# A hybrid decoder layer on one core: the lo parts of all weight tiles, on VectorE or on GpSimd

## The chip, the cores and the metric

The kernel runs on one core of a Trainium2 chip. The engines that matter are TensorE (in the profile PE for its matmuls and PEld for its weight loads), VectorE (DVE), ScalarE (ACT), GpSimd (POOL) and SyncE (SP), which here issues most DMAs; names that end in q are an engine's queue. The metric is the device time of one execution in microseconds. Before the change three runs took 1840.11, 1841.65 and 1845.51 us; the median is 1841.65.

## What is computed

One layer with three token mixers side by side, on 2048 tokens of width 1024, in fp32. Cut to what matters:

```python
hn = rms_norm(x, pre_norm_w)
u = hn @ w_in                                   # 1024 -> 5392 columns, split
y_ssd  = ssd_mixer(z, xbc, dt, ...)             # conv of 4 taps, chunked state space, gated norm
y_conf = conformer_conv(conf_in, ...) * silu(conf_gate)   # conv of 31 taps, layer norm
y_attn = sliding_window_attention(q, k, v, ...) * silu(attn_gate)
y = concatenate([y_ssd, y_conf, y_attn])        # 2048 columns
h = x + rms_norm(y @ w_out, post_norm_w)
out = h + (p @ ple_proj) * sigmoid(h @ ple_gate)
```

## The kernel before

Everything is kept transposed: 128 channels on the partitions, 512 tokens (one of four chunks) in a row. The four large products (w_in, w_out, ple_gate, ple_proj) are made in a reduced-precision fp32 format of TensorE, called fp32r in the profile. To keep fp32 accuracy both factors are split in two: hi is the value rounded to fp32r, lo is what the rounding left. A product is then three matmuls, hi by lo, lo by hi and hi by hi, added up in one PSUM tile (lines 443 to 445, 1048 to 1050, and 207 to 209).

Weights come in tiles of 128 rows by 1024 numbers (512 KB; for ple_proj 128 by 256). `load_w` fetches one into a staging buffer `wst`, of which there are two (line 196, a DMA on SyncE's queue), has ScalarE write `whi` (line 190, a CAST) and VectorE subtract to get `wlo` (line 191, inside the helper `split`). There are five buffers each for `whi` and `wlo`. A `wst` buffer is free again when the subtraction has read it; only then can SyncE issue the load of the tile after next. `split` serves the activations too, which is why line 191 also stands for `al` and `bl` in the profile. The one tile named dt has its own code (`dt_tile`, lines 459 to 461) with its own small subtraction on VectorE.

The program has three stages, which follow each other on TensorE:

- Stage 1, to about 1240 us: two halves of two chunks each. In each half the 17 units of work in a list (A attention, C conformer, S state space, G a new group) load their two or three weight tiles, project both chunks with them (`proj`), and leave the rest of their work to generators that are advanced between the projections. The conformer's convolution needs 30 VectorE instructions for each tile of two chunks (line 691, one per tap), dealt out between the others.
- Stage 2, to about 1619 us: for each of four chunks 16 weight tiles of w_out, 24 matmuls per tile; beside them the norms of the next chunk (`stats`, `prep`) and, after each chunk, `post` (lines 328 to 330), which normalises the result, adds x and writes h to DRAM.
- Stage 3, the gate loop, from line 1080 on: for each of four chunks eight turns; a turn loads a ple_gate tile and a ple_proj tile, makes 24 and 6 matmuls, and ends with a tanh on ScalarE (line 1090), two VectorE instructions (1091, 1092) and the store (1093). With two staging buffers and these two kinds of tile in turn, each kind has one buffer. `prep_h` brings and splits the next chunk of h beside it.

The order in which each engine goes through its instructions is fixed when the program is built: a scheduler sets it from the code, the buffers and its own estimates of duration. On the chip every engine goes through its list in order, and a waiting instruction holds up all that stand behind it.

Of the kernel before, what the change touches and what calls it, by code (L numbers as in the profile page):

```python
# [8 lines left out]
F32 = mybir.dt.float32  # L9
# [3 lines left out]
ALU = mybir.AluOpType  # L13
# [48 lines left out]
def hybrid_block_kernel(  # L62
# [16 lines left out]
    V, A, G, PE = nc.vector, nc.scalar, nc.gpsimd, nc.tensor  # L79
# [109 lines left out]
    def split(hi, lo, src):  # L189
        A.copy(hi, src)  # L190
        V.tensor_tensor(out=lo, in0=src, in1=hi.bitcast(F32), op=ALU.subtract)  # L191

    def load_w(src, nk=KD):

        st = wp.tile([P, KD, P], F32, tag="wst", name="wst", bufs=2)
        nc.sync.dma_start(out=st[:, 0:nk, :], in_=src)
        hi = wp.tile([P, KD, P], F32R, tag="whi", name="whi", bufs=5)
        lo = wp.tile([P, KD, P], F32R, tag="wlo", name="wlo", bufs=5)
        split(hi[:, 0:nk, :], lo[:, 0:nk, :], st[:, 0:nk, :])
        return hi, lo  # L200

    def mm3(out, w, acts, nk, start=True, stop=True):
# [143 lines left out]
    with ExitStack() as c1:  # L346
# [103 lines left out]
        def wtile(name):  # L450
            return load_w(w_in[TIDX[name]])
# [573 lines left out]
    with ExitStack() as c2:  # L1025
        ring_b["pool"] = c2.enter_context(tc.tile_pool(name="ringb", bufs=4))
        op = c2.enter_context(tc.tile_pool(name="op", bufs=5))
        while pending:
            advance()
        for c in range(NCHUNK):  # L1030
# [7 lines left out]
            for n, (dp, kg) in enumerate(steps):  # L1038
                if kg == 0:
                    pjs[dp] = [ps("pp") for _ in range(2)]  # L1040
                pj = pjs[dp]
                hi, lo = load_w(w_out[dp, kg])
                for kk in range(4):
                    yh, yl = ys[4 * kg + kk]
# [32 lines left out]
        for c in range(NCHUNK):  # L1077
            cs = slice(c * TC, (c + 1) * TC)
            hs, pr = HS[c]
            for d in range(KD):  # L1080
                wg = load_w(w_gate[d])
                wl = load_w(w_ple[d], 2)
                hr = t512("hr")
                nc.sync.dma_start(out=hr, in_=h_d[d, :, cs])
                pg = ps("pp")
                mm3(pg, wg, lambda k: hs[k], KD)
                pe = ps("pp")
                mm3(pe, wl, lambda k: pr[k], 2)
                gt = t512("gt")
                A.activation(gt, pg, AF.Tanh, scale=0.5)  # L1090
                V.scalar_tensor_tensor(out=gt, in0=gt, scalar=1.0, in1=pe, op0=ALU.add, op1=ALU.mult)
                V.scalar_tensor_tensor(out=gt, in0=gt, scalar=0.5, in1=hr, op0=ALU.mult, op1=ALU.add)
                nc.sync.dma_start(out=outT[d, :, cs], in_=gt)
                advance()
                if d == 3 and c + 1 < NCHUNK:
                    pending.append(prep_h(c + 1, *HS[c + 1]))
# [108 lines left out]
```

## Time and profile before

| | before |
|---|---|
| median of three runs | 1841.65 us |
| profiled execution | 1850.51 us, its span 1848.7 us |
| TensorE clock granted, mean | 0.994 |
| weight subtractions on VectorE | 214 |
| other work of GpSimd | four memsets at the start |

A row of a group reads: line, engine, operation, tile written <- tiles read, shapes, count | busy time, mean ns of one | idle time of the engine just before, and who ended it. A row of waits reads: engine, its tile and line <- who released it: us in total, times, longest. A row of the timeline reads: start, duration, engine and line, operation, tiles, and in brackets the engine's idle time before it and its releaser. A row of the view by windows has the stretch, its length, then the busy time and count of TensorE's matmuls, its weight loads, VectorE, ScalarE and GpSimd, the granted clock, the DMA engines' share and GB/s.

### The profile page before, as it was taken

How to read it: one execution, taken by the hardware profiler on the slowest of the kernel's cores; microseconds unless marked ns; L12 is line 12 of the kernel's file. 1: busy time of each engine (PE TensorE's matmuls, PEld its weight loads, DVE VectorE, ACT ScalarE, POOL GpSimd, SP SyncE). 2: the span in 40 equal slices, each digit the busy share in tenths (PEclk: the TensorE clock that was granted, in tenths of full speed). 3: DMA queues.
4: the chain of work that ended last, by engine and by line, in shares of the span. 5: the costliest groups of instructions: out<-in, count | busy, mean ns of one | idle time of the engine just before them, and what ended most of it. 6: DMA issues, size and time to landing. Idle time of an engine off the chain costs nothing.

```text
span 1848.7 us, 25168 instructions
## 1 busy us (share of the span) xinstructions
PE 1810.7 (98%) x9386; PEld 1461.6 (79%) x9386; DVE 1385.1 (75%) x2400; ACT 818.6 (44%) x1565; POOL 0.2 (0%) x4
## 2 busy tenths in 40 slices
PE   6999999999999999999999999999999999999998
PEld 5877787787888778878788887877888788887887
DVE  6859769759869875976975996988777867466543
ACT  5525425524726542542653371465444444343331
POOL 0000000000000000000000000000000000000000
PEclk9999999999999999999999999999999999999999
DMA  7443233224433433333332332346677766578554
GB/s 234 132 133 98 80 102 96 61 78 106 171 112 111 121 102 104 91 87 89 100 115 76 101 99 87 82 145 230 214 242 236 245 228 199 202 240 280 189 188 131
DMA packets 118982, 265.09 MB, mean 143 GB/s; under 512 B 12619, under 2 KB 20428, under 8 KB 118860
## 3 DMA queue, kind: packets, MB, share of 16 engines
q1 hardware_dynamic: 108428, 246.65, 40.9%
q10 hardware_dynamic: 10432, 16.83, 4.1%
q8 instruction: 74, 1.21, 0.3%
q14 instruction: 48, 0.39, 0.1%
HBM read 205.05 MB, written 39.50 MB: 132 GB/s over the span
## 4 chain that ended last, share of the span: by engine, by line
PE 78%; DMA 8%; DVE 6%; ACT 4%; issue 2%; ACTq 1%; SPq 0%; DVEq 0%
PE ps_pp L443 15%; PE ps_pp L444 14%; PE ps_pp L445 14%; PE ps_pp L1048 4%; PE ps_pp L1049 4%; PE ps_pp L1050 4%; PE ps_pp L208 3%; PE ps_pp L209 3%; PE ps_pp L207 3%; PE ps_m L766 2%; PE ps_y L940 2%; PE ps_y L838 2%; DMA Ab<-acs_d 2%; PE ps_y L937 2%; PE ps_m L816 1%
## 5 line engine op out<-in xcount | busy, mean ns | idle before, releaser
L443 PE MATMUL ps_pp<-al,whi 128*128 128x512 f32 x1344 | 536.6, 400 | 13.6 <-DVE al L393 10.4
L444 PE MATMUL ps_pp<-ah,wlo 128*128 128x512 f32 x1344 | 534.5, 398 | 0.0
L445 PE MATMUL ps_pp<-ah,whi 128*128 128x512 f32 x1344 | 534.1, 397 | 0.0
L191 DVE TENSOR_TENSOR wlo<-wst,whi 128x1024 fp32r<-128x1024 f32 x214 | 234.1, 1102 | 179.8 <-ACT whi L190 179.4
L443 PEld LDWEIGHTS ps_pp<-al,whi 128*128 128x128 f32 x1344 | 254.4, 189 | 73.1 <-DVE al L393 10.4
L190 ACT CAST whi<-wst 128x1024 fp32r<-128x1024 f32 x214 | 202.9, 951 | 242.0 <-DMA wst<-in_w_gate_dram 86.1
L691 DVE SCALAR_TENSOR_TENSOR acc<-gl,par_sb,acc 128x1024 f32<-128x1024 f32 x240 | 307.3, 1280 | 2.3
L444 PEld LDWEIGHTS ps_pp<-ah,wlo 128*128 128x128 f32 x1344 | 254.6, 189 | 55.8 <-issue 6.5
L445 PEld LDWEIGHTS ps_pp<-ah,whi 128*128 128x128 f32 x1344 | 254.5, 189 | 54.4 <-issue 4.9
L489 DVE SCALAR_TENSOR_TENSOR cv<-raw,par_sb,cv 128x512 f32<-128x512 f32 x144 | 107.6, 747 | 22.7 <-ACT cv L487 22.0
L208 PE MATMUL ps_pp<-ah,wlo 128*128 128x512 f32 x256 | 100.2, 391 | 3.7 <-DVE wlo L191 3.7
L1048 PE MATMUL ps_pp<-bl,whi 128*128 128x512 f32 x256 | 101.5, 399 | 0.6 <-ACT whi L190 0.6
L1048 PE MATMUL ps_pp<-al,whi 128*128 128x512 f32 x256 | 100.4, 393 | 0.7 <-DVE al L191 0.7
L1049 PE MATMUL ps_pp<-bh,wlo 128*128 128x512 f32 x256 | 101.1, 395 | 0.0
L1050 PE MATMUL ps_pp<-bh,whi 128*128 128x512 f32 x256 | 100.7, 394 | 0.0
L207 PE MATMUL ps_pp<-al,whi 128*128 128x512 f32 x256 | 100.1, 391 | 0.6 <-ACT whi L190 0.5
L1049 PE MATMUL ps_pp<-ah,wlo 128*128 128x512 f32 x256 | 100.1, 391 | 0.0
L1050 PE MATMUL ps_pp<-ah,whi 128*128 128x512 f32 x256 | 100.0, 390 | 0.0
L209 PE MATMUL ps_pp<-ah,whi 128*128 128x512 f32 x256 | 99.7, 389 | 0.0
L796 ACT ACTIVATE S<-S,nm 128x256 f32<-128x256 f32 (+1 forms) x128 | 62.8, 492 | 80.0 <-DVE nm L782 74.6
L903 ACT ACTIVATE Ab<-Ab,acs 128x128 f32<-128x128 f32 x256 | 82.4, 391 | 0.4
L937 PE MATMUL ps_y<-Ab,xd 128*64 128x128 f32 x512 | 61.5, 282 | 2.0 <-issue 2.0
(235 smaller groups left out, 2592.1 us busy)
## 6 DMA issues: line engine op xcount, KB each, us to landing
wst<-in_w_in_dram SPq DMA_DIRECT2D x88, 512.0 KB, 3.5
wst<-in_w_out_dram SPq DMA_DIRECT2D x64, 512.0 KB, 5.1
Ab<-acs_d SPq DMA_DIRECT2D x64, 256.0 KB, 4.5
ysd<-y_d SPq DMA_DIRECT2D x32, 512.0 KB, 5.5
wst<-in_w_gate_dram SPq DMA_DIRECT2D x32, 512.0 KB, 3.5
gl<-in_xT_dram SPq DMA_DIRECT2D x16, 512.0 KB, 4.0
qh<-qh ACTq DMA_DIRECT2D x64, 128.0 KB, 2.4
ql<-ql ACTq DMA_DIRECT2D x64, 128.0 KB, 2.4
```

The costliest lines, as they stand in the source:

```text
L190: A.copy(hi, src)
L191: V.tensor_tensor(out=lo, in0=src, in1=hi.bitcast(F32), op=ALU.subtract)
L207: PE.matmul(out, lhsT=hi[:, k, :], rhs=al, start=start and k == 0, stop=False)
L208: PE.matmul(out, lhsT=lo[:, k, :], rhs=ah, start=False, stop=False)
L209: PE.matmul(out, lhsT=hi[:, k, :], rhs=ah, start=False, stop=stop and k == nk - 1)
L443: PE.matmul(o_, lhsT=hi[:, k, :], rhs=al, start=k == 0, stop=False)
L444: PE.matmul(o_, lhsT=lo[:, k, :], rhs=ah, start=False, stop=False)
L445: PE.matmul(o_, lhsT=hi[:, k, :], rhs=ah, start=False, stop=k == KD - 1)
L691: V.scalar_tensor_tensor(out=acc, in0=gl[:, k:k + 2 * TC], scalar=pc("ccw", j * 31 + k), in1=acc, op0=ALU.mult, op1=ALU.add)
L1048: PE.matmul(pj[dd], lhsT=hi[:, i, :], rhs=yl, start=first, stop=False)
L1049: PE.matmul(pj[dd], lhsT=lo[:, i, :], rhs=yh, start=False, stop=False)
L1050: PE.matmul(pj[dd], lhsT=hi[:, i, :], rhs=yh, start=False, stop=last)
```

## The change

In `load_w` the call of `split` is replaced by its two parts, and the second one is issued by GpSimd. The cast stays on ScalarE. The activations' splits and dt's small subtraction stay on VectorE.

```diff
@@ -196,7 +196,8 @@
         nc.sync.dma_start(out=st[:, 0:nk, :], in_=src)
         hi = wp.tile([P, KD, P], F32R, tag="whi", name="whi", bufs=5)
         lo = wp.tile([P, KD, P], F32R, tag="wlo", name="wlo", bufs=5)
-        split(hi[:, 0:nk, :], lo[:, 0:nk, :], st[:, 0:nk, :])
+        A.copy(hi[:, 0:nk, :], st[:, 0:nk, :])
+        G.tensor_tensor(out=lo[:, 0:nk, :], in0=st[:, 0:nk, :], in1=hi[:, 0:nk, :].bitcast(F32), op=ALU.subtract)
         return hi, lo
```

One line is added, so every line behind it has a number higher by one in the changed kernel; the subtraction is line 200 there and the cast 199.

The scheduler sets the order anew. The first place is VectorE in the first half of stage 1, at the second attention unit; the `acc` rows are taps of the convolution, the rows on `nm`, `es`, `mx` and `S` belong to the softmax, and `wlo_2750` is the lo tile of a weight that a later unit uses. Before:

```order
L805 TENSOR_SCALAR S_2218<-S_2218,rd_2242 128x256 x2
L782 TENSOR_SCALAR nm_2284<-mx_2282 128x4 [waits DVE_49]
L691 SCALAR_TENSOR_TENSOR acc_2075<-gl_1883,par_sb_79,acc_2075 128x1024
L785 TENSOR_TENSOR es_2298<-nm_2284,par_sb_79 128x4 [waits DVE_49]
L191 TENSOR_TENSOR wlo_2750<-wst_2747,whi_2749 128x1024 [waits DMAHW6_49]
L691 SCALAR_TENSOR_TENSOR acc_2075<-gl_1883,par_sb_79,acc_2075 128x1024 [waits DVE_49]
```

The same place now:

```order
L806 TENSOR_SCALAR S_2218<-S_2218,rd_2242 128x256 x2
L771 ISA S_2281,mx_2282<-ps_m_2280,bias_2109,par_sb_79 128x256
L771 ISA mx_2282 128x1
L692 SCALAR_TENSOR_TENSOR acc_2075<-gl_1883,par_sb_79,acc_2075 128x1024
L783 TENSOR_SCALAR nm_2284<-mx_2282 128x4 [waits DVE_49]
L692 SCALAR_TENSOR_TENSOR acc_2075<-gl_1883,par_sb_79,acc_2075 128x1024 [waits DVE_49]
L786 TENSOR_TENSOR es_2298<-nm_2284,par_sb_79 128x4 [waits DVE_49]
```

The subtraction is gone from VectorE's list, and the taps have moved up between the softmax's small instructions.

The second place is the gate loop near its end, on VectorE and GpSimd (`wlo_15315` and `wlo_15321` are the lo tiles of a gate and a ple weight, `gt` is the result of an earlier turn). VectorE before:

```order
L191 TENSOR_TENSOR wlo_15315<-wst_15312,whi_15314 128x1024 [waits DMAHW4_49,Activation_49]
L191 TENSOR_TENSOR wlo_15321<-wst_15318,whi_15320 128x256 [waits DMAHW6_49,PE_49,Activation_49]
L1091 SCALAR_TENSOR_TENSOR gt_15256<-gt_15256,ps_pp_15249 128x512 [waits DMAHW7_49,PE_49]
L1092 SCALAR_TENSOR_TENSOR gt_15256<-gt_15256,hr_15222 128x512 [waits DMAHW5_49,DVE_49]
L191 TENSOR_TENSOR wlo_15366<-wst_15363,whi_15365 128x1024 [waits DMAHW0_49,Activation_49]
```

GpSimd now, where nothing else stands in the list:

```order
L200 TENSOR_TENSOR wlo_15315<-wst_15312,whi_15314 128x1024 [waits DMAHW4_49,Activation_49]
L200 TENSOR_TENSOR wlo_15321<-wst_15318,whi_15320 128x256 [waits DMAHW6_49,PE_49,Activation_49]
L200 TENSOR_TENSOR wlo_15366<-wst_15363,whi_15365 128x1024 [waits DMAHW0_49,Activation_49]
L200 TENSOR_TENSOR wlo_15372<-wst_15369,whi_15371 128x256 [waits DMAHW2_49,PE_49,Activation_49]
L200 TENSOR_TENSOR wlo_15417<-wst_15414,whi_15416 128x1024 [waits DMAHW4_49,Activation_49]
```

The subtractions keep their order and their waits for the load and the cast; they no longer stand between the rows on `gt`, which alone are left on VectorE.

The third place is SyncE's queue in the same loop (`out_0_dram<-gt` stores a result, `hr` is a chunk of h). Before:

```order
L1093 DMA out_0_dram<-gt_15205 128x512 [waits DMAHW7_49,DVE_49]
L196 DMA wst_15363<-in_w_gate_dram 128x1024 [waits DMAHW4_49,DVE_49]
L1084 DMA hr_15273<-h_d_76 128x512 [waits DMAHW1_49]
L196 DMA wst_15369<-in_w_ple_dram 128x256 [waits DMAHW6_49,DVE_49]
L1093 DMA out_0_dram<-gt_15256 128x512 [waits DMAHW3_49,DVE_49]
```

Now:

```order
L1094 DMA out_0_dram<-gt_15205 128x512 [waits DMAHW7_49,DVE_49]
L196 DMA wst_15363<-in_w_gate_dram 128x1024 [waits DMAHW4_49,Pool_49]
L1085 DMA hr_15273<-h_d_76 128x512 [waits DMAHW1_49]
L196 DMA wst_15369<-in_w_ple_dram 128x256 [waits DMAHW6_49,Pool_49]
L1094 DMA out_0_dram<-gt_15256 128x512 [waits DMAHW3_49,DVE_49]
```

The order is the same there; the weight loads wait for GpSimd in place of VectorE.

## The prediction

> **What bounds the kernel now.** I read the page's busy times first, then its chain of work that ended last, then the waits of TensorE.
>
> ```profile
> PE 1810.7 (98%) x9386; PEld 1461.6 (79%) x9386; DVE 1385.1 (75%) x2400; ACT 818.6 (44%) x1565; POOL 0.2 (0%) x4
> PE 78%; DMA 8%; DVE 6%; ACT 4%; issue 2%; ACTq 1%; SPq 0%; DVEq 0%
> ```
>
> TensorE is occupied in 98% of the span and makes up 78% of the chain. A faster VectorE can bring only what TensorE loses by waiting. The waits of TensorE, grouped by who released it, have 15 rows; their sum is 32.8 us, and these are six of them, the first and the last included:
>
> ```profile
> PE ps_pp L443 <- DVE al L393: 10.4, 1, 10.4
> PE ps_pp L208 <- DVE wlo L191: 3.7, 4, 1.7
> PE ps_m L159 <- DVE csum L263: 3.6, 1, 3.6
> PE ps_y L940 <- DVE H L918: 3.5, 6, 1.2
> PE ps_pp L443 <- DVE al L191: 3.2, 1, 3.2
> ...
> PE ps_pp L207 <- ACT whi L190: 0.5, 1, 0.5
> ...
> PE ps_m L766 <- DVE mx L770: 0.2, 1, 0.2
> ```
>
> The 10.4 us are the start, before the first activation pair is split; only 22.4 us of waits lie behind it. A weight's lo part is the releaser in 3.7 us, a cast's hi part in 0.5 us of the last loop. So the gain is small whatever VectorE sheds, and the question is what a slower subtraction does to tiles that TensorE will need.
>
> **What is removed.** The groups of line 191 for the weight tiles, kept apart by shape, and the cast in front of them:
>
> ```profile
> L191 DVE TENSOR_TENSOR wlo<-wst,whi 128x1024 fp32r<-128x1024 f32 x182 | 221.9, 1222 | 160.4 <-ACT whi L190 160.1
> L190 ACT CAST whi<-wst 128x1024 fp32r<-128x1024 f32 x182 | 190.7, 1048 | 237.7 <-DMA wst<-in_w_gate_dram 86.1 <-PE ps_pp L445 45.1 <-PE ps_pp L1050 43.6
> L191 DVE TENSOR_TENSOR wlo<-wst,whi 128x256 fp32r<-128x256 f32 x32 | 13.5, 421 | 19.4 <-ACT whi L190 19.3
> ```
>
> VectorE loses 182 subtractions of 1222 ns and 32 of 421 ns, 235.4 us together, and 179.4 us in which it stood in front of one of them until the cast was done. All of this lies beside TensorE's work, so its removal is worth nothing by itself.
>
> **What a subtraction costs on GpSimd.** The profile has no elementwise GpSimd row: its four instructions are memsets that take 0.2 us together. The low end is VectorE's own 1.22 us. For the value I take two passes at the cast's rate, one for each source read, 2 x 1.048 = 2.1 us: the cast is the nearest row for an engine that reads one source. The high end adds one VectorE instruction of the commonest kind with two SBUF sources, in case GpSimd must stand behind it:
>
> ```profile
> L691 DVE SCALAR_TENSOR_TENSOR acc<-gl,par_sb,acc 128x1024 f32<-128x1024 f32 x240 | 307.3, 1280 | 2.3
> ```
>
> That is 2.1 + 1.28 = 3.4 us. The Trainium skill, page GPSIMD Engine Reference, section Performance versus the Vector engine, has 4497 ns for a two-input add of 2048 fp32 elements, 2293 ns on VectorE. Halved, its VectorE figure is 1.15 us where this trace has 1.22; its GpSimd figure would be an estimate of 2.25 us, with which the sum of the last loop below would come to +11.8 us in place of +7.6.
>
> **The last loop, where the time is made.** In the gate loop (from 1618.8 us on) the two staging buffers alternate between a gate tile and a ple tile. So a gate load waits for the subtraction of the gate tile before it, and four things form a ring: load, cast, subtraction, next load. One turn of it, from the timeline of SyncE's queue, ScalarE and VectorE (start, duration):
>
> ```profile
> 1758.98 0.33 SPq L196 DMA_DIRECT2D wst<-in_w_gate_dram  x1
> 1762.99 1.05 ACT L190 CAST whi<-wst 128x1024 fp32r<-128x1024 f32 x1 [4.50 <-DMA wst<-in_w_gate_dram]
> 1764.07 1.56 DVE L191 TENSOR_TENSOR wlo<-wst,whi 128x1024 fp32r<-128x1024 f32 x2 [3.45 <-ACT whi L190]
> 1765.32 0.33 SPq L196 DMA_DIRECT2D wst<-in_w_gate_dram  x1
> ```
>
> The load takes 4.01 us to the cast, the cast 1.05, the subtraction 1.22 (the row merges it with the ple tile's 0.42), and 0.03 us after it the next load is issued: 6.34 us. TensorE needs this for one turn (30 weight loads lie between these two):
>
> ```profile
> 1835.01 0.19 PEld L208 LDWEIGHTS ps_pp<-ah,wlo 128*128 128x128 f32 x1
> 1841.81 0.19 PEld L208 LDWEIGHTS ps_pp<-ah,wlo 128*128 128x128 f32 x1
> ```
>
> 6.80 us. The ring is only just faster than TensorE, and the change puts 2.1 - 1.22 = 0.88 us into each turn. What it has in hand is read at gate tile 3, and the turns from the issue times of gate tiles 3, 7, 8, 18 and 31:
>
> ```profile
> 1627.37 1.22 DVE L191 TENSOR_TENSOR wlo<-wst,whi 128x1024 fp32r<-128x1024 f32 x1
> 1640.11 0.19 PEld L208 LDWEIGHTS ps_pp<-ah,wlo 128*128 128x128 f32 x1
> ...
> 1621.77 0.33 SPq L196 DMA_DIRECT2D wst<-in_w_gate_dram  x1
> ...
> 1650.92 0.33 SPq L196 DMA_DIRECT2D wst<-in_w_gate_dram  x1
> ...
> 1669.52 0.35 SPq L196 DMA_DIRECT2D wst<-in_w_gate_dram  x1
> ...
> 1739.11 0.33 SPq L196 DMA_DIRECT2D wst<-in_w_gate_dram  x1
> ...
> 1820.27 0.33 SPq L196 DMA_DIRECT2D wst<-in_w_gate_dram  x1
> ```
>
> Tile 3 is ready 1640.11 - 1628.59 = 11.5 us ahead; with two longer subtractions behind it, 9.7. Tiles 3 to 7 turn in 29.15 / 4 = 7.29 us, now 8.17, and lose 1.37 each: 4.2 left at tile 7. Between 7 and 8 lies the one clear gain. Before, the subtraction of tile 7 stood on VectorE behind the normalisation of the previous stage, which waited for a broadcast row:
>
> ```profile
> 1657.13 0.75 DVE L328 SCALAR_TENSOR_TENSOR o_sb<-o_sb,par_sb,rb__14023 128x512 f32<-128x512 f32 x1 [3.08 <-DMA rb__14023<-row]
> ...
> 1668.24 1.22 DVE L191 TENSOR_TENSOR wlo<-wst,whi 128x1024 fp32r<-128x1024 f32 x1
> 1669.51 0.19 PEld L208 LDWEIGHTS ps_pp<-ah,wlo 128*128 128x128 f32 x1 [2.09 <-DVE wlo L191]
> ```
>
> On GpSimd nothing stands ahead of it, so this turn costs what those before it do, some 8.2 us: 2.8 in hand at tile 8. The ten turns from 8 to 18 took 69.59 / 10 = 6.96, now 7.84: ten times 1.04 is 10.4, of which 7.6 are TensorE's wait. The thirteen to tile 31 took 81.16 / 13 = 6.24, now 7.12: thirteen times 0.32 is 4.2. In all 11.8 us of new waits, and the old ones (3.7 + 0.5) go: **+7.6 us**. By the low end nothing is added and 4.2 go: -4.2. By the high end (2.16 us per turn) it is 3.4 + 2.7 + 23.2 + 20.8 - 4.2 = +46 us.
>
> On SyncE's queue the next hr load and the out store stand behind the waiting gate load; the out store goes to DRAM and nobody waits for it, and hr is needed only behind the turn's last matmul. On GpSimd only other subtractions queue.
>
> **Stages 1 and 2.** By stage, in the view by windows (start, first projections, output projection, gate loop):
>
> ```profile
> 0.00:50.00 50.00, 35.89 (x140) 27.83 (x141) 32.32 (x70) 27.02 (x44) 0.20 (x4) 0.94 0.71 233
> 50.00:1240.00 1190.00, 1181.15 (x6568) 946.41 (x6567) 956.95 (x1769) 536.24 (x1195) 0.00 (x0) 1.00 0.34 102
> 1240.00:1618.80 378.80, 372.78 (x1713) 306.91 (x1713) 276.39 (x398) 180.26 (x217) 0.00 (x0) 0.99 0.67 224
> 1618.80:1848.70 229.90, 220.88 (x970) 180.46 (x968) 119.40 (x165) 75.11 (x111) 0.00 (x0) 1.00 0.63 207
> ...
> 150.00:200.00 50.00, 49.99 (x315) 38.86 (x313) 46.78 (x97) 30.96 (x84) 0.00 (x0) 1.00 0.30 96
> ...
> 250.00:300.00 50.00, 49.97 (x261) 40.49 (x260) 49.26 (x83) 15.51 (x44) 0.00 (x0) 1.00 0.38 104
> ...
> 1150.00:1200.00 50.00, 49.68 (x275) 40.71 (x273) 49.82 (x97) 19.55 (x53) 0.00 (x0) 1.00 0.34 90
> ```
>
> The ring does not bind here. In stage 2 a tile feeds 24 matmuls, 24 x 0.227 = 5.4 us, and the two buffers give it two such times, 10.9 us, against 5.1 for the load, 1.05 and 2.1: no wait, and the cover ends only at a subtraction of 4.7 us. In stage 1 a tile is loaded long ahead and then stands in VectorE's queue; here it is from 425.5 us, where its cast ends, to 435.1:
>
> ```profile
> 424.48 1.04 ACT L190 CAST whi<-wst 128x1024 fp32r<-128x1024 f32 x1
> ...
> 435.12 1.22 DVE L191 TENSOR_TENSOR wlo<-wst,whi 128x1024 fp32r<-128x1024 f32 x1
> ```
>
> On GpSimd such a tile is ready earlier, not later, at about 427.6. The cost, if any, is on VectorE: should an instruction with two SBUF sources stand still while GpSimd reads, stage 2 has 276.4 - 65 x 1.2 = 198 us of VectorE plus 64 x 2.1 = 134, 88% of it, and stage 1 957 - 103 + 85 x 2.1 = 1033 us, 87%. That fits on average but not in stretches like 250 to 300 us, with VectorE at 49.26 of 50 and three subtractions: 49.26 - 3.66 + 6.3 = 51.9. Eight 50-us stretches have VectorE at 46.78 or more, the first and the last of them in the fence; if each overflow cost TensorE 1 us it would be 8, and as the next stretch can take up some of it I count half, **+4 us** (between -7, half of the VectorE waits behind the start, and +8). At the start the second lo tile comes 0.88 us later; the 3.2 us wait for al, quoted above, hides it, and without that cover it costs 0.88.
>
> **The sum.** 7.6 + 4 = 11.6. The profiled execution took 1850.5 us (span 1848.7 and 1.8 around it), 8.9 above the median 1841.65 of three runs. It would become 1862; on the median I put the same 11.6: **1853 us**.
>
> **Rivals.** *VectorE set free gains.* If GpSimd subtracts in about 1.22 us and holds up nothing, the last loop gives -4.2, and half of the 14 us of waits for other late VectorE results go (3.6, 3.5 and 3.2 us are the largest of them): 1841.65 - 4.2 - 7 = 1830. For it speaks the 179.4 us in which VectorE stood for casts, against it that no row shows GpSimd as fast as VectorE. It decides below 1.22 + (6.80 - 6.24) = 1.78 us per subtraction, where the ring's quiet turns stay under TensorE's 6.80. *Everything hides.* A subtraction around 1.8 us loses in the busy turns what tile 7 gains: within 0.3% (5.5 us, about what a measurement of this kernel can tell from no change). *The two engines shut each other out.* Each subtraction waits for a running VectorE instruction, 3.4 us in all: 1841.65 + 46 + 4 = 1892. The busy VectorE (75%) speaks for it, its lighter load in the gate loop (119.4 of 229.9) against. The Trainium skill, page SBUF — State Buffer, section Who interferes with whom, says that a VectorE instruction with two SBUF inputs contends with a GpSimd instruction that reads SBUF, one blocking the other for its whole length. No run so far shows it, since GpSimd does nothing here; by that rule this rival would be the likelier one in stage 2.
>
> **Chances.** Forecast (1847.2 to 1868) 0.48; shut out (1868 to 1892) 0.14; hides 0.22; gains 0.16. Slower by over 0.3%: 0.48 + 0.14 = 0.62; within: 0.22; faster: 0.16. The range goes from the low end of the loop alone, 1841.65 - 4.2 = 1837, to the high end, 1892, and leaves out most of the gain.
>
> **What would show it.** The GpSimd group of line 200 near 2.1 us, and issue times of gate loads some 7.1 us apart after tile 18; TensorE's waits at line 208 on GpSimd near 12 us in the last loop; line 328 no longer ahead of a subtraction. VectorE's line 691 at 1.28 us would say that it isn't held, a longer mean that it is. Wrong would be the forecast if the gate loads keep 6.3 us, or if TensorE's new waits lie in stages 1 and 2.

## The result, and the profile after

| | before | changed |
|---|---|---|
| median of four runs | 1842.76 us (1840.11 to 1845.51) | 2005.65 us (2001.15 to 2010.9) |
| span of the profiled execution | 1848.7 us | 2005.0 us |
| TensorE clock granted, mean | 0.994 | 0.973 |

The changed kernel is slower by a ratio of 1.0885 (95% interval 1.0852 to 1.0917), outside the predicted range. The profiled execution before took 1850.5 us, some 8 us above its median, so spans and stages differ by 156.3 us in what follows, where the medians differ by 162.9. The changed kernel's busy times, from its page, and the chain of work that ended last:

```profile
PE 1849.8 (92%) x9386; PEld 1480.4 (74%) x9386; DVE 1404.7 (70%) x2186; ACT 818.0 (41%) x1565; POOL 500.0 (25%) x218
PE 44%; DVE 31%; DMA 9%; ACT 6%; issue 6%; POOL 3%; SPq 0%; ACTq 0%; DVEq 0%; POOLq 0%
```

VectorE has 214 instructions fewer, and its busy time has risen, from 1385.1 to 1404.7 us. It now makes up 31% of the chain, where it was 6%. The waits of TensorE, summed over all releasers, come to 150.3 us (32.8 before), and VectorE released 129.8 of them (28.5 before). These are seven of the largest rows:

```profile
PE ps_m L817 <- DVE S L806: 20.1, 17, 1.9
PE ps_m L911 <- DVE xw L897: 18.7, 10, 2.4
PE ps_m L159 <- DVE osum L1070: 16.6, 3, 6.2
PE ps_m L767 <- DVE mx L771: 11.5, 14, 1.3
PE ps_m L608 <- DVE da L597: 11.4, 2, 6.0
PE ps_pp L444 <- DVE al L394: 10.2, 1, 10.2
PE ps_pp L209 <- POOL wlo L200: 10.2, 15, 1.9
```

Only the last one is a wait for a lo tile. The others, apart from the start (L394, which was there before), are small matmuls of the softmax, the state space and the norms that need a VectorE result. By windows (start, the rest of stage 1, stage 2, gate loop):

```profile
0.00:50.00 50.00, 35.22 (x137) 27.29 (x138) 30.82 (x63) 26.98 (x44) 12.19 (x9) 0.97 0.65 217
50.00:1345.70 1295.70, 1202.39 (x6573) 956.98 (x6572) 984.01 (x1689) 539.27 (x1197) 220.38 (x85) 0.98 0.31 95
1345.70:1763.40 417.70, 385.66 (x1710) 315.60 (x1709) 282.65 (x331) 176.54 (x215) 159.97 (x64) 0.95 0.60 201
1763.40:2005.00 241.60, 226.56 (x970) 180.56 (x968) 107.20 (x105) 75.18 (x111) 107.43 (x60) 0.99 0.60 197
```

Stage 1 has grown by 105 us (1240.5 to 1345.7), stage 2 by 39, the gate loop by 11.7. The lower clock is part of it: 2.7% of 2005.0 us against 0.6% of 1848.7 is some 43 us more, which shows as longer matmuls (PE's busy time is 39.1 us longer). The record of the granted clock has it in 18 stretches at half clock, 110.1 us together (6 stretches and 24.6 us before); in them a 128x512 matmul starts every 427 ns in the median, elsewhere every 227. The 39.1 us and the 117.5 us of new waits account, to within 0.3 us, for the 156.3 us between the spans.

What happens to VectorE is seen in a single instruction. The timeline of GpSimd, then of VectorE, at 312 us:

```profile
312.64 2.43 POOL L200 TENSOR_TENSOR wlo<-wst,whi 128x1024 fp32r<-128x1024 f32 x1 [11.95 <-ACT whi L199]
...
312.73 2.37 DVE L800 TENSOR_SCALAR rd<-rd 128x4 f32<-128x4 f32 x1
315.01 0.68 DVE L500 SCALAR_TENSOR_TENSOR ag<-ag,ps_pp 128x512 f32<-128x512 f32 x1
315.61 0.17 DVE L801 RECIPROCAL rd<-rd 128x4 f32<-128x4 f32 x1
```

The VectorE instruction on 128x4 numbers starts 0.09 us after the subtraction and ends at 315.10, 0.03 us behind its end (315.07). In the kernel before, its group took 166 ns in the mean; here it took 2.37 us. The groups that carry this through the kernel, VectorE's taps, that small instruction and the gate loop's last one, and GpSimd's subtractions:

```profile
L692 DVE SCALAR_TENSOR_TENSOR acc<-gl,par_sb,acc 128x1024 f32<-128x1024 f32 x240 | 338.1, 1409 | 14.0 <-ACT acc L690 11.1
...
L800 DVE TENSOR_SCALAR rd<-rd 128x4 f32<-128x4 f32 x32 | 13.7, 427 | 0.3
...
L1093 DVE SCALAR_TENSOR_TENSOR gt<-gt,hr 128x512 f32<-128x512 f32 x32 | 43.6, 1364 | 2.2 <-DMA hr<-h_d 1.3
...
L200 POOL TENSOR_TENSOR wlo<-wst,whi 128x1024 fp32r<-128x1024 f32 x182 | 465.3, 2558 | 1469.1 <-ACT whi L199 1391.1 <-DVE CBm L532 24.2 <-PE ps_m L767 21.8
L200 POOL TENSOR_TENSOR wlo<-wst,whi 128x256 fp32r<-128x256 f32 x32 | 35.3, 1103 | 25.2 <-ACT whi L199 21.8 <-PE ps_m L159 3.3
```

The taps took 1280 ns before, the gate loop's instruction 690. VectorE's instructions other than the weights' subtractions took 229.5 us longer, summed one by one (1294.4 before, 1523.9 now): nearly what was taken off VectorE, 235.4 us, came back as time in which one of its instructions stood still beside GpSimd. Such a standstill is called a **hold** below. VectorE's load is thus about what it was, and the kernel takes 163 us more. The experiments are about that difference.

### The profile page after: what moved, and what is told of

The parts are those of the page before. It is cut to its first block, busy times and chain, and to the rows that moved or that the text cites. A ratio compares the mean times of both kernels' runs of the same rounds, so it can differ in the third digit from the quotient of the medians.

```text
span 2005.0 us, 25341 instructions
## 1 busy us (share of the span) xinstructions
PE 1849.8 (92%) x9386; PEld 1480.4 (74%) x9386; DVE 1404.7 (70%) x2186; ACT 818.0 (41%) x1565; POOL 500.0 (25%) x218
## 4 chain that ended last, share of the span: by engine, by line
PE 44%; DVE 31%; DMA 9%; ACT 6%; issue 6%; POOL 3%; SPq 0%; ACTq 0%; DVEq 0%; POOLq 0%
DVE acc L692 11%; PE ps_pp L445 8%; PE ps_pp L446 8%; PE ps_pp L444 8%; DMA wst<-in_w_gate_dram 5%; POOL wlo L200 3%; PE ps_pp L1049 3%; PE ps_pp L1050 3%; PE ps_pp L1051 3%; DVE cv L490 2%; ACT whi L199 2%; PE ps_y L941 2%; PE ps_y L938 2%; DVE S L771 1%; PE ps_m L911 1%
## 5 line engine op out<-in xcount | busy, mean ns | idle before, releaser
L200 POOL TENSOR_TENSOR wlo<-wst,whi 128x1024 fp32r<-128x1024 f32 x214 | 499.8, 2340 | 1494.3 <-ACT whi L199 1412.9
L444 PE MATMUL ps_pp<-al,whi 128*128 128x512 f32 x1344 | 538.9, 401 | 13.8 <-DVE al L394 10.2
L692 DVE SCALAR_TENSOR_TENSOR acc<-gl,par_sb,acc 128x1024 f32<-128x1024 f32 x240 | 338.1, 1409 | 14.0 <-ACT acc L690 11.1
L444 PEld LDWEIGHTS ps_pp<-al,whi 128*128 128x128 f32 x1344 | 256.2, 191 | 73.1 <-DVE al L394 10.2
L490 DVE SCALAR_TENSOR_TENSOR cv<-raw,par_sb,cv 128x512 f32<-128x512 f32 x144 | 122.3, 849 | 25.8 <-ACT cv L488 25.0
L209 PE MATMUL ps_pp<-ah,wlo 128*128 128x512 f32 x256 | 102.6, 401 | 10.2 <-POOL wlo L200 10.2
L1092 DVE SCALAR_TENSOR_TENSOR gt<-gt,ps_pp 128x512 f32<-128x512 f32 x32 | 21.9, 683 | 90.3 <-ACT gt L1091 49.8
L678 DVE SCALAR_TENSOR_TENSOR gl<-gth,ps_pp 128x512 f32<-128x512 f32 x16 | 11.0, 688 | 105.2 <-PE ps_pp L446 94.7
```

What stands on the lines that cost most here:

```text
L200: G.tensor_tensor(out=lo[:, 0:nk, :], in0=st[:, 0:nk, :], in1=hi[:, 0:nk, :].bitcast(F32), op=ALU.subtract)
L209: PE.matmul(out, lhsT=lo[:, k, :], rhs=ah, start=False, stop=False)
L444: PE.matmul(o_, lhsT=hi[:, k, :], rhs=al, start=k == 0, stop=False)
L490: V.scalar_tensor_tensor(out=v, in0=raw[:, k:k + TC], scalar=pc("scw", ci * 4 + k), in1=v, op0=ALU.mult, op1=ALU.add)
L692: V.scalar_tensor_tensor(out=acc, in0=gl[:, k:k + 2 * TC], scalar=pc("ccw", j * 31 + k), in1=acc, op0=ALU.mult, op1=ALU.add)
```

## The experiments

Three causes were possible: VectorE held by GpSimd ("Held VectorE"), the scheduler's new order ("New order"), and lo tiles that come 1.2 us later ("Late lo tiles"). To keep the order apart, the program is built twice where a diff says so: `program(X)` builds it with the weights subtracted by X (V VectorE, G GpSimd, N nobody) and returns the order of each engine's instructions; the second build is chained to that order, without any new wait. The subtractions themselves stay free to go where the scheduler puts them. All medians and ratios are against the kernel before, timed on the same chip beside them (1841.57, 1840.66, 1841.43 and 1838.71 us in the four groups).

| run | us | ratio (95%) | stages 1, 2, 3 | VectorE held by | TensorE waits | clock |
|---|---|---|---|---|---|---|
| before | 1841.6 | | 1240, 378, 230 | 0 | 32.8 | 0.994 |
| changed | 2005.65 | 1.0885 (1.0852 to 1.0917) | 1346, 418, 242 | 229.5 | 150.3 | 0.973 |
| 1 G, order of before | 1992.17 | 1.0831 (1.0789 to 1.0873) | 1325, 426, 250 | 236.1 | 133.1 | 0.972 |
| 2 V, order of changed | 1968.26 | 1.07 (1.0655 to 1.0745) | 1337, 395, 235 | 0 | 128.8 | 0.970 |
| 3 V, idle G beside | 1982.21 | 1.076 (1.0728 to 1.0793) | 1321, 418, 234 | 199.0 | 118.6 | 0.979 |
| 4 none, order of changed | 1829.64 | 0.9935 (0.9911 to 0.9958) | 1237, 371, 224 | 0 | 26.4 | 0.994 |
| 5 G at VectorE's turn | 1950.61 | 1.0592 (1.0557 to 1.0627) | 1289, 405, 252 | 204.8 | 102.9 | 0.986 |
| 6 G in quarters | 1965.12 | 1.0664 (1.062 to 1.0708) | 1284, 414, 270 | 155.4 | 109.0 | 0.977 |
| 7 G in eighths | 2006.46 | 1.0904 (1.0864 to 1.0944) | 1288, 428, 296 | 110.7 | 140.1 | 0.966 |
| 8 V, G copies beside | 1886.39 | 1.0243 (1.0208 to 1.0277) | 1261, 392, 230 | 87.0 | 59.9 | 0.992 |
| 9 V twice, order of before | 1929.16 | 1.0463 (1.0424 to 1.0503) | 1290, 411, 231 | 0 | 83.8 | 0.980 |
| 10 none, order of before | 1827.53 | 0.9922 (0.9894 to 0.995) | 1229, 369, 229 | 0 | 21.8 | 0.997 |
| 11 G in the gate loop only | 1860.23 | 1.0108 (1.0077 to 1.0138) | 1230, 378, 249 | 27.9 | 40.2 | 0.995 |
| 12 changed, PSUM operand | 2007.91 | 1.0902 (1.0861 to 1.0942) | 1345, 421, 245 | | 153.7 | 0.974 |
| 13 V twice, own order | 1861.64 | 1.0126 (1.0106 to 1.0147) | 1249, 383, 227 | 0 | 40.8 | 0.993 |
| 14 G in planned room, at turn | 1929.25 | 1.0476 (1.0442 to 1.0511) | 1277, 404, 247 | 191.1 | 85.5 | 0.982 |

"Held by" is what VectorE's instructions took longer than the same ones in the kernel before, summed, in us (in runs 3 and 8 with what its own subtractions took longer, 49.4 and 24.5).

### Hold or order: runs 1 to 4

Run 1:

```diff
-    nc, _ = program("G")
+    _, order = program("V")
+    nc, _ = program("G", order)
```

> GpSimd subtracts all the weights' lo parts, as in the changed kernel, but the instructions of TensorE, VectorE, ScalarE and SyncE stand in the order that the kernel before has (VectorE's subtractions are simply missing from its row). Held VectorE (each GpSimd subtraction keeps VectorE from working until it ends, and TensorE waits for VectorE's late results, in whatever order): 1950 to 2010 us, nearly all of the loss stays. New order (the loss comes from where the scheduler puts TensorE's small matmuls now that VectorE looks freer, right behind the VectorE results that they need): 1845 to 1880 us. Late lo tiles (only the 2.4 us for 1.22 us count, in the gate loop): about 1855 us.

1992.17 us: nearly all of the loss stands in the old order. As VectorE has the same list in both kernels, each instruction can be set beside itself. 168 VectorE instructions with all operands in SBUF began while a GpSimd subtraction ran; 158 of them were lengthened, by 239.8 us in all. 69 began in such a time with an operand in PSUM, and none was lengthened. Of 96 that were running when GpSimd began, one was. The whole growth of 236 us lies in those 158. TensorE's waits for VectorE are 105.7 us in this run (28.5 before), those for GpSimd 10.8. The Trainium skill, page SBUF — State Buffer, section Who interferes with whom, states it so: a VectorE instruction with two SBUF inputs contends with a GpSimd instruction that reads SBUF, and whoever issues first blocks the other for the whole instruction. These counts agree with it. They go beyond two inputs too: 17 of the 158, 16 TENSOR_SCALARs and a COPY, read one tensor (and at most a scalar per partition beside it).

Run 2:

```diff
+    _, order = program("G")
+    nc, _ = program("V", order)
```

> VectorE subtracts, as in the kernel before, but all the other instructions of the four engines stand in the order of the changed kernel. Held VectorE: 1843 to 1870 us, since nothing holds VectorE any more. New order: 1920 to 2005 us, since the order that costs the time is kept. Late lo tiles: 1843 to 1850 us.

1968.26 us, where "Held VectorE" expected 1843 to 1870: an order planned for a VectorE without subtractions is bad when VectorE makes them. TensorE waits 49.7 us for one VectorE result (the state H) alone. Run 4 has the same order with nobody subtracting:

```diff
-        lo = wp.tile([P, KD, P], F32R, tag="wlo", name="wlo", bufs=5)
-        G.tensor_tensor(out=lo[:, 0:nk, :], in0=st[:, 0:nk, :], ...)
+        lo = lo0        # one tile of zeros, written once
...
+    _, order = program("G")
+    nc, _ = program("N", order)
```

> The order of the changed kernel on all engines, but no engine subtracts: every weight tile has one tile of zeros for its lo part (the product hi + lo of the weights is left out down to hi; the number of matmuls is kept). Held VectorE: 1815 to 1845 us, as the order does no harm and VectorE is 235 us freer than before with no hold. New order: 1880 to 1990 us, since TensorE still stands right behind VectorE's results. Late lo tiles: 1830 to 1843 us, as the gate loop's wait for lo tiles is gone.

1829.64 us. The new order does no harm by itself; runs 2 and 4 together say that it does harm when VectorE is late. Run 3 keeps the old order and all that TensorE waits for, and adds GpSimd work that nobody needs:

```diff
+        scr = wp.tile([P, KD - 1, P], F32, tag="scr", name="scr", bufs=1)
+        G.tensor_tensor(out=scr[...], in0=hi[...], in1=hi[...], op=ALU.subtract)
```

> The kernel before in its own order, VectorE subtracting; GpSimd in addition runs one subtraction for each weight tile (hi minus hi, 7 of the 8 blocks of 128 columns, 2.1 us by 7/8 of the 2.40 us that one takes undisturbed) into a scratch tile that nobody reads. No engine waits for it. Held VectorE: 1940 to 2010 us, as slow as the changed kernel or worse, since VectorE has its own subtractions as well as the holds. New order: 1843 to 1850 us, since the order is that of before. Late lo tiles: 1843 to 1850 us, since the lo tiles come as early as before.

1982.21 us, though nobody reads what GpSimd makes. With the counts of run 1 this shows the hold as the main cause; the changed kernel, with its new order, takes 13 us more than run 1. Stages 1 and 2 lose 81 and 40 us in run 3, where VectorE makes the lo tiles, so GpSimd's slower subtraction is not needed for the loss there.

### Which instructions are held, and by which: runs 8 and 12

Run 8 is run 3 with `G.tensor_copy(out=scr[...], in_=hi[...])`.

> As the third experiment (the kernel before in its own order, with idle GpSimd work beside it), but GpSimd copies the hi tile, one operand instead of two, 7 of 8 blocks. If GpSimd holds VectorE whenever it reads and writes its own side of the memory: 1920 to 1985 us, as the third experiment's 1982 us in proportion to the copy's own length (taken at 1 to 2 us). If only GpSimd's two-operand work does: 1835 to 1855 us.

1886.39 us: a one-operand copy holds VectorE as well: of 127 instructions with all operands in SBUF that began beside a copy (VectorE's own subtractions not counted) 116 were lengthened. It takes 1466 ns in the mean for the tile where run 3's subtraction took 2242, and costs 46 us where that cost 141. The cost falls by more than the length; why is not shown.

Run 12:

```diff
-                V.scalar_tensor_tensor(out=gt, in0=gt, scalar=1.0, in1=pe, ...)
-                V.scalar_tensor_tensor(out=gt, in0=gt, scalar=0.5, in1=hr, ...)
+                V.scalar_tensor_tensor(out=pe, in0=gt, scalar=1.0, in1=pe, ...)
+                V.scalar_tensor_tensor(out=gt, in0=pe, scalar=0.5, in1=hr, ...)
```

> The changed kernel in its own order, with one edit in the gate loop: the first of the two VectorE instructions on gt writes its result over its PSUM operand, and the second reads it there, so that it has one operand in PSUM and one in SBUF where it had both in SBUF. In the changed kernel the second took 1364 ns in the mean (690 in the kernel before), the first, with a PSUM operand, was not held. If only VectorE instructions with all operands in SBUF are held: 0.68 to 0.80 us in the mean, and VectorE's time in the gate loop falls by some 20 us. If any instruction can be held: it stays at 1.2 to 1.4 us. The whole takes 1995 to 2006 us either way, as TensorE waits for these results nowhere.

The two groups in run 12, in the view by lines:

```profile
L1102 DVE SCALAR_TENSOR_TENSOR ps_pp<-gt,ps_pp 128x512 f32<-128x512 f32 x32 | 22.2, 692 | 110.5 <-ACT gt L1100 87.9 <-PE ps_pp L218 11.8 <-PE ps_pp L219 6.6
...
L1103 DVE SCALAR_TENSOR_TENSOR gt<-ps_pp,hr 128x512 f32<-128x512 f32 x32 | 22.1, 690 | 3.5 <-DMA hr<-h_d 2.6
```

690 ns in place of 1364, the longest 693, though 21 of the 32 began beside a GpSimd subtraction: with one operand in PSUM the same arithmetic runs unheld. The time stays, as TensorE waits for it nowhere.

### When and how long: runs 5 to 7

Run 5 adds, for each weight tile, a wait of GpSimd's subtraction for the VectorE instruction that stood ahead of VectorE's own one:

```diff
+    _, order, turn = program("V")
+    nc, _, _ = program("G", order, turn)
...
+            for n, k in enumerate(turn):
+                tc.add_manual_dep(subtraction[n], vector_instruction[k], Sync, ...)
```

> As the first experiment (GpSimd subtracts, all other instructions in the order of the kernel before), and each GpSimd subtraction in addition waits for the VectorE instruction behind which VectorE's own subtraction of that tile stood in its row. So GpSimd cannot start ahead of VectorE results that came first in the kernel before; a subtraction can still hold what VectorE does next. Ill-timed holds (the loss comes because GpSimd starts as soon as a tile is rounded, ahead of VectorE work that TensorE waits for, while VectorE's own subtraction came after it): 1845 to 1900 us. Length of a hold (what counts is that one hold lasts up to 2.4 us, wherever it begins): 1940 to 1995 us, near the first experiment's 1992 us.

1950.61 us: 110 us above the kernel before, where run 1 is 151 above it. Some 41 us, then, go with holds that cut in ahead of what stood first; the rest stays. It is a net figure, as the subtractions now come later: TensorE's waits for GpSimd rise from 10.8 to 23.2 us. Runs 6 and 7 cut run 1's subtraction (here 6):

```diff
-        G.tensor_tensor(out=lo[:, 0:nk, :], ...)
+        for k in range(0, nk, 2):
+            G.tensor_tensor(out=lo[:, k:k + 2, :], in0=st[:, k:k + 2, :], ...)
```

> As the first experiment, but each subtraction of 128x1024 is cut in four of 128x256 (0.73 us each undisturbed, 2.9 us together; the 128x256 tiles of the gate loop stay whole). Length of a hold: a held VectorE instruction gets in after one piece, 1890 to 1940 us, as the mean hold falls from 1.5 us to about 0.5. Ill-timed holds: about the same, 1890 to 1950 us. Total of GpSimd's time (VectorE gets in only when a whole tile is done, or is held by every piece in turn): 2000 to 2040 us, since a tile takes 2.9 us instead of 2.4.

> As the last one with eight pieces of 128x128 for a tile (0.45 us each by the line through 0.73 us at 256 and 2.40 us at 1024 columns; 3.6 us together). Length of a hold: 1870 to 1910 us, below the quarters. Total of GpSimd's time: 2030 to 2080 us. If the pieces' own starts cost more than the shorter holds give back, it lies above the quarters while both lie under 1992 us.

1965.12 and 2006.46 us, worse than either expectation for shorter holds. The subtractions' group in run 1:

```profile
L209 POOL TENSOR_TENSOR wlo<-wst,whi 128x1024 fp32r<-128x1024 f32 x214 | 496.4, 2327 | 1493.1 <-ACT whi L207 1345.7
```

In run 6, with four pieces to a tile:

```profile
L212 POOL TENSOR_TENSOR wlo<-wst,whi 128x256 fp32r<-128x256 f32 x760 | 720.6, 980 | 1237.8 <-ACT whi L207 1158.4
```

In run 7, with eight:

```profile
L212 POOL TENSOR_TENSOR wlo<-wst,whi 128x128 fp32r<-128x128 f32 x1520 | 941.5, 657 | 1062.3 <-ACT whi L207 940.8
```

In stage 1 shorter holds do help: 1325 us fall to 1284 and 1288. But GpSimd's time nearly doubles, from 496 to 941 us. In the gate loop the next load waits for the last piece: TensorE's waits there for the cast of a tile sum to 23.4 us in run 6 and 43.4 in run 7, and the stage grows from 250 to 270 and 296. Two effects, one against the other.

### What room VectorE has: runs 9, 10, 13 and 14

> As the fourth experiment (no subtraction at all, one tile of zeros for every lo part), but in the order of the kernel before. It fills the last cell beside the two orders. If the changed kernel's order is what makes use of a freer VectorE: 1836 to 1843 us, above the fourth's 1830. If the order matters little once VectorE is free: 1826 to 1835 us.

Run 10 (`program("N", order)` after `program("V")`): 1827.53 us. VectorE's own 235 us of subtractions thus cost 14 us in the kernel before. Moving them off VectorE can gain no more than that in this order (12 us in run 4's); other orders were not tried. Run 9 has VectorE subtract a second time in place of run 3's GpSimd:

```diff
+        V.tensor_tensor(out=scr[...], in0=hi[...], in1=hi[...], op=ALU.subtract)
```

> The kernel before in its own order, and VectorE itself does what GpSimd did in the third experiment: behind the real subtraction one more of 7 blocks (hi minus hi, some 1.07 us) into a scratch tile that nobody reads, placed by the scheduler where VectorE is free. GpSimd does nothing. If what counts is only how long VectorE is kept from other work (206 us more here, against 150 us of holds in the third experiment): 1940 to 2000 us. If what counts is that GpSimd holds VectorE at moments that no order accounts for, while VectorE's own work stands where its row leaves room: 1845 to 1890 us.

1929.16 us, between the two expectations: 211 us more of its own work cost 88. Run 13 is the same program with the order that the scheduler gives it, that is, with this work in its plan:

> As the ninth experiment (VectorE subtracts, and subtracts once more into a scratch tile; GpSimd does nothing), but the scheduler sets the order with this work in its plan, instead of the order of the kernel before. If the ninth lost its 88 us because VectorE has no room for 211 us more: 1915 to 1940 us again. If it lost them because that order was planned without the extra work: 1845 to 1885 us.

1861.64 us, 23 above the kernel before. The page's busy times of run 9:

```profile
PE 1842.3 (95%) x9386; PEld 1479.4 (77%) x9386; DVE 1564.2 (81%) x2614; ACT 818.3 (42%) x1565; POOL 0.2 (0%) x4
```

And of run 13:

```profile
PE 1811.8 (98%) x9386; PEld 1458.4 (78%) x9386; DVE 1557.3 (84%) x2614; ACT 822.3 (44%) x1565; POOL 0.2 (0%) x4
```

The same work, and TensorE at 98% with VectorE at 84%: VectorE has the room, if the order knows of it. Run 14 puts GpSimd's subtractions in that room, in run 13's order and at run 5's kind of turn (`order` and `turn` from `program` with V twice):

> GpSimd subtracts as in the changed kernel, and all other instructions stand in the order that the thirteenth experiment has, which was planned with 2.3 us of VectorE's time for each weight tile, about what a GpSimd subtraction (2.4 us) holds it at most; as in the fifth, each subtraction waits for the VectorE instruction behind which VectorE's own first subtraction stood. If the loss is a matter of an order that leaves no room at the right places: 1850 to 1900 us. If GpSimd's holds hit TensorE's results wherever the order puts them: 1925 to 1965 us, as the fifth's 1951.

1929.25 us, 21 below run 5 and still 90 above the kernel before timed beside it, as expected if the holds hit TensorE's results wherever the order puts them. Its TensorE waits 52.1 us for VectorE (run 5: 69.5) and 22.9 for GpSimd.

### The gate loop by itself: run 11

```diff
-        e = G
+        e = G if stage == 3 else V
```

> GpSimd subtracts in the gate loop alone (32 tiles of 128x1024 and 32 of 128x256), VectorE everywhere else, all in the order of the kernel before. If the loss is the sum of what each stage loses by itself: the gate loop is 20 us longer, as in the first experiment, and the rest is as before: 1855 to 1866 us. If the lo tiles' later arrival in the loop is the only cost there, it is the prediction's 7.6 us: 1846 to 1852 us.

1860.23 us, 18.8 above the kernel before, and the loop's length in the profile (249 for 230) says the same; stages 1 and 2 lose nothing. So the loop loses by itself what it loses in run 1 (250). Run 3, with the holds but with VectorE's lo tiles, lost 4 us in the loop, which leaves some 15 to the later tiles. TensorE waits 9.9 us for GpSimd, and 5.6 us once, for the cast of gate tile 8. The load of that tile did not wait for a subtraction, as the timelines of GpSimd and of SyncE's queue show with the subtraction of tile 7 and the loads of tiles 7 and 8:

```profile
1648.15 2.39 POOL L211 TENSOR_TENSOR wlo<-wst,whi 128x1024 fp32r<-128x1024 f32 x1 [2.84 <-ACT whi L209]
...
1643.43 0.33 SPq L206 DMA_DIRECT2D wst<-in_w_gate_dram  x1
...
1660.65 0.43 SPq L342 DMA_DIRECT2D h_d<-xres  x1
1661.13 0.54 SPq L1097 DMA_DIRECT2D hr<-h_d  x1
1661.77 1.06 SPq L206 DMA_DIRECT2D wst<-in_w_gate_dram  x1
```

Tile 7's buffer is read by 1650.54, but in the old order of SyncE's queue the load of tile 8 stands behind stores of h (line 342) from stage 2, and is issued 18.34 us after that of tile 7. GpSimd has only 109.5 us of work in this run, and it costs 19.

## Why the prediction was wrong

**Stages 1 and 2** are the step that failed: "if each overflow cost TensorE 1 us it would be 8, and as the next stretch can take up some of it I count half, +4 us (between -7 ... and +8)". It measured 145 us (105 + 39). The prediction had the hold in view and asked whether VectorE's time plus GpSimd's fits into 50-us stretches. That is a count of capacity, and run 13 shows that by capacity there was room: VectorE at 84% costs 23 us. But a hold is not work that an order has placed. In run 1 the 158 holds of 1.5 us in the mean (239.8 / 158) fell on whatever VectorE was about to do, and TensorE stands in a fixed order close behind short chains of VectorE results, as the rows L806 to L817 and L897 to L911 of the changed kernel show. About the same amount of time on VectorE thus cost 14 us where it was planned (run 10 against before), 88 where it was unplanned work of its own (run 9), and 151 as holds (run 1, of which 20 lie in the gate loop with its later tiles).

**The lower clock** had no term in the sum. About 43 of the 156 us between the profiled spans are lost in it. It goes with the waits: runs 4 and 10, which wait 22 to 26 us, have 0.994 and 0.997, run 7 with 140 us has 0.966. That the waits bring the clock down is likely by these rows, but was not tried by itself.

**"All of this lies beside TensorE's work, so its removal is worth nothing by itself"** was nearly right: runs 4 and 10 gain 12 and 14 us with no subtraction at all. What came in the place of the removed work was the whole matter.

**The duration on GpSimd** was taken as 2.1 us and measured about 2.40 undisturbed (the median of the 182 is 2.41, the row at 312.64 us 2.43), inside its bounds of 1.22 and 3.4. The estimate of 2.25 us worked out from the Trainium skill's page GPSIMD Engine Reference, section Performance versus the Vector engine, was nearer.

**The gate loop** was right in mechanism and near in size: +7.6 forecast, +11.7 measured, with 10.2 us of waits on GpSimd at line 209 for the 11.8 forecast. The tiles' reserve went as worked out: at tile 7 the lo tile was 5.0 us ahead of TensorE (4.2 forecast), at tile 8 2.9 (2.8), and at tile 10 it was gone. Two things in this were luck. With a subtraction of 2.40 us the same working gives 20.7 us of new waits and +16.5 in all, further off than the 11.8 and +7.6 that came of 2.1. And the gain between tiles 7 and 8 needed more than that "on GpSimd nothing stands ahead of it": the load of tile 8 was issued 7.06 us after that of tile 7 here (18.60 before), but 18.34 in run 11, where GpSimd subtracts too and SyncE's queue has the old order. The gain came with the new order of that queue. SyncE's queue also gives the length of a turn near the end, from two issues of gate loads seven turns apart:

```profile
1935.43 0.33 SPq L196 DMA_DIRECT2D wst<-in_w_gate_dram  x1
...
1986.30 0.33 SPq L196 DMA_DIRECT2D wst<-in_w_gate_dram  x1
```

50.87 / 7 = 7.27 us, where 7.1 was forecast with a subtraction of 2.1.

**The rival "the two engines shut each other out"** named the mechanism, and priced the wrong side of it. It took GpSimd as the one that waits, 3.4 us per subtraction, and put the price in the gate loop's ring. GpSimd's mean is 2558 ns, 0.16 us over its undisturbed time, some 29 us over all 182; VectorE waits 229.5 us, and what that costs lies mostly in stages 1 and 2. Line 692 at 1409 ns is the sign of it that the prediction had given, and "if TensorE's new waits lie in stages 1 and 2" is where it called itself wrong.

What stays open is how the 90 us that run 14 still loses divide between holds and late tiles outside the gate loop, where it waits 9.9 us for GpSimd (22.9 less 13.0 at the loop's line), and whether an order that knew each hold's moment could do better. No run beat the kernel before with the whole computation in it. Leaving VectorE's subtractions out altogether brought 12 and 14 us in the two orders tried.

## What to carry to other kernels

Before work goes from VectorE to GpSimd, count not the time that VectorE sheds but the time that GpSimd will read and write SBUF, here 500 us for 235, and look at which VectorE results TensorE stands closely behind: each of them that has all operands in SBUF can come nearly a whole GpSimd instruction late (2.2 us for one of 2.4). A busy share of 75% does not say that an engine can take unplanned delay; about the same load cost 14 us where the order had it and 151 as holds. Where the two must overlap, a PSUM operand on VectorE's side keeps an instruction out of the hold.

## What the hardware showed that was not expected

- The hold strikes the smallest instructions for the full length: 128x4 with one SBUF operand took 2.37 us for 0.17. Not every instruction with its operands in SBUF is held. In the changed kernel the RECIPROCAL behind it never began beside a subtraction; in runs 1, 3, 6, 7, 8 and 14 it did 17 times, and took 163 to 178 ns each time. One of these in run 14, in the timelines of GpSimd and VectorE:

```profile
619.62 2.41 POOL L209 TENSOR_TENSOR wlo<-wst,whi 128x1024 fp32r<-128x1024 f32 x1 [18.42 <-issue]
...
619.73 0.18 DVE L815 RECIPROCAL rd<-rd 128x4 f32<-128x4 f32 x1
```

- Cutting a GpSimd instruction is dear: the median piece of run 7 took 465 ns, or 8 x 0.465 = 3.7 us for a tile that took 2.4 undisturbed, and the mean piece 657 ns. GpSimd is held in its turn: the 644 pieces that began while a VectorE instruction with its operands in SBUF was running took 907 ns in the median, the others 461.
- The granted clock fell where TensorE waits more: in stage 2 it was 0.95 (0.99 before), while TensorE's time not busy in the stage rose from 378.80 - 372.78 = 6 us to 417.70 - 385.66 = 32 us.
